# Hybrid trunk on one core: level operands of the recurrence kept side by side, the small-tile scores gathered into two visits a round, the first microseconds reordered

## The chip, the core and the metric

The kernel runs on one core of a Trainium2 chip. The metric is the device time of one execution in microseconds. Three runs of the kernel before took 986.7 to 988.48 us, median 987.43. One more execution was recorded by the hardware profiler; all rows below are of that one.

## What is computed

Two decoder layers over 256 tokens of 2048 features. The change touches the first, a gated linear recurrence (HGRN2) with 16 heads of 128:

```python
def hgrn2_mixer(h, w_in, lb, head_gain, w_out):
    proj = (h @ w_in).astype(jnp.float32).reshape(B, S, 4, HGRN_HEADS, HGRN_HEAD_DIM)
    q, f_pre, v, z = proj[:, :, 0], proj[:, :, 1], proj[:, :, 2], proj[:, :, 3]
    log_f = jnp.log(lb + (1.0 - lb) * jax.nn.sigmoid(f_pre))
    k = (1.0 - lb) * jax.nn.sigmoid(-f_pre)
    o = chunk_gated_recurrence(q * HGRN_HEAD_DIM ** -0.5, k, v, log_f)
    o = rms_norm(o, head_gain) * jax.nn.silu(z)
    return o.reshape(B, S, HGRN_WIDTH).astype(h.dtype) @ w_out
```

Within the recurrence the output at token t is the sum over s <= t of (q_t . decay(s, t) . k_s) v_s, where decay(s, t) is the product of the gates between s and t, one per feature. The second layer (sparse attention with three branches) and the final norm are not touched.

## The kernel before

**Main products.** Every weight matrix is streamed once from HBM in pieces of 128 x 1024 numbers (L26). SyncE issues the loads into six buffers; ScalarE casts a piece to fp32r (`hi`, L132), VectorE subtracts that from the raw piece (`lo`, L142), and TensorE multiplies hi and lo parts with hi and lo parts of the activations (L150 token-major, three products a term; L173 and L175 feature-major). A piece gives twelve token-major products of 512 columns, or eight feature-major pairs.

**The order of work.** It is written out by hand. `plan` lists the pieces of all chunks; `flush` (L252) walks through it: a piece's products, and before and after them one `advance()`, which takes one step of every open generator in `steps` (a `yield` ends a step). So a generator makes two steps a piece, and its instructions stand in each engine's queue between those of the pieces. `prefetch` emits casts, splits and loads some pieces ahead. In the first chunk, whose pieces have `before` set, `start_piece` (L240) does that, with `split_x` (L318): it transposes a 256-column block of x on TensorE and makes its hi and lo part on ScalarE and VectorE. `flush` begins with `start_piece(2)` and asks in the middle of piece i for piece i + 3. Pieces 0 and 1 hold one row block of the weights each and share the first block of x; from piece 2 on each piece needs a block of its own, the last being piece 8.

**Before flush** (L1110 to L1132): seven small loads of parameters into `prow` and `rb` on POOL's queue, x and the first pieces on SyncE's, a transpose of the norm gains `gn` (L1125), `start_piece(0)`, ten transposes of the identity into an unused bank (L1129), then the generators `setup()` (masks, bias table, lower bounds `lb` and `oml`) and `norm_x()`.

**A round of the recurrence** has four heads, worked as two pairs (a = 0, 1), and streams four chunks of eight pieces: f, q, v, z. At the end of each f chunk `f_take` (L423) moves the four result banks out; the first time it calls `open_hg` (L581), which drains all open generators and hands the memory of the start to the recurrence, so `gather`'s copies wait for the last reader of that memory.

**Scores** (`scores_of`, L473), started for both pairs when q is done, so during the v chunk. It goes over levels h = 1, 2, 4 ... 128. A level's products give the scores between neighbouring blocks of h tokens; then q of every second block and k of every other are multiplied in place with the gates `T` of the neighbouring block (L514, L515) and the gates pairwise with each other (L519). For h up to 16 (L491) the products are 32 x 32 tiles, placed with `tile_position` in four column groups of the array, sixteen for each pair and level; the first level takes 64 moving columns (two levels of q at once). Level 32 (L497) has eight products in two of the four column groups, level 64 (L502) four products with a 64-column stationary, level 128 (L506) two with full tiles. A level's products come at the end of a piece, its multiplications at the beginning of the next, so a round has eight visits of TensorE to them, each with both pairs one behind the other. VectorE picks the results by masks (L523, L526); ScalarE and POOL copy them to `ST` (L529, L533, L535, L537), which `mix_of` (L540) multiplies with v after the z chunk.

Matmul records of the trace: a float32 product leaves two loads and two matmuls.

Of the kernel before, what the change touches and what calls it, by code (L numbers as in the profile page):

```python
# [8 lines left out]
F32 = mybir.dt.float32  # L9
# [7 lines left out]
P = 128  # L17
D = 2048
S = 256
KT = D // P  # L20
NH = 16
HD = 128
# [23 lines left out]
def kernel(ctx: ExitStack, tc: tile.TileContext, x, norm_gains, final_gain, rel_bias,  # L46
                             hgrn_lb, hgrn_w_in, hgrn_head_gain, hgrn_w_out, nsa_w_in, nsa_pe_k, nsa_pe_v,
                             phi_k_w1, phi_k_b1, phi_k_w2, phi_v_w1, phi_v_b1, phi_v_w2, nsa_w_out, out):
    nc = tc.nc
# [190 lines left out]
    def start_piece(i):  # L240
        while state["hi"] <= min(i, len(plan) - 1):
            j = state["hi"]
            ch, kts, _ = plan[j]
            if ch and ch["before"]:
                ch["before"](kts)
            prefetch(j, 1)
            while state["lo"] <= j:
                emit_lo(state["lo"])
                state["lo"] += 1
            prefetch(j, 0)  # L250

    def flush():  # L252
        start_piece(2)
        finished = None
        for i, (ch, kts, last) in enumerate(plan):
# [10 lines left out]
            emit_products(i, (lambda: start_piece(i + 3)) if starting else None)  # L266
# [42 lines left out]
    xt = sp.tile([P, 2, D], F32, name="xt")  # L309
    ssqp = sp.tile([P, 2, 4], F32, name="ssqp")  # L310
# [39 lines left out]

    def setup():
# [26 lines left out]
        nc.gpsimd.tensor_copy(xf, xi)  # L378
        yield
# [7 lines left out]
        yield  # L387
        yield
        yield
# [83 lines left out]
    def scores_of(a):  # L473
        Fg, Kg, QQ = HG["F", a], HG["K", a], HG["Q", a]
        ST, S32 = HG["ST", a], HG["S32", a]
        nc.vector.tensor_mul(QQ[:, 1], QQ[:, 0], Fg)
        TT = HG["pool"].tile([P, 512], F32, tag=f"TT{a}", name="TT")
        T, off = Fg, 0
        yield
        lev = []  # L480
        for l, h in enumerate((1, 2, 4, 8, 16, 32, 64, 128)):
            if h <= 16:
                i0, i1 = (0, 2) if l == 0 else (l + 1, l + 2)
                if h in (1, 8):
                    lev.append(aux_bank().rearrange("p (l j t) -> p l j t", l=4, j=4))
                dst = lev[i0 // 4]
                q0 = 0 if l == 0 else 1
                for j in range(4):
                    for b in range(4):
                        cs = slice(j * P + 32 * b, j * P + 32 * b + 32)  # L490
                        nc.tensor.matmul(dst[32 * b:32 * b + 32, i0 % 4:(i1 - 1) % 4 + 1, j, :], Kg[:, cs],  # L491
                                         QQ[:, q0:2, cs], start=True, stop=True, tile_position=(0, 32 * b))
            elif h == 32:
                for j in range(4):
                    for b in (0, 2):
                        c = j * P + 32 * b
                        nc.tensor.matmul(lev[1][32 * b:32 * b + 32, 2, j, :], Kg[:, c:c + 32],  # L497
                                         QQ[:, 1, c + 32:c + 64], start=True, stop=True, tile_position=(0, 32 * b))
            elif h == 64:
                far = aux_bank()  # L500
                for j in range(4):
                    nc.tensor.matmul(far[0:64, j * 64:j * 64 + 64], Kg[:, j * P:j * P + 64],  # L502
                                     QQ[:, 1, j * P + 64:j * P + 128], start=True, stop=True)
            else:
                for hh in range(2):
                    nc.tensor.matmul(far[:, 256 + hh * P:256 + (hh + 1) * P], Kg[:, hh * S:hh * S + P],  # L506
                                     QQ[:, 1, hh * S + P:(hh + 1) * S], start=True, stop=True)
            yield
            if h < 128:
                n = 512 // (2 * h)  # L510
                Tv = T.rearrange("p (n two) -> p n two", two=2)
                Qv = QQ[:, 1].rearrange("p (n two h) -> p n two h", two=2, h=h)
# [652 lines left out]
```

## Time and profile before

| | us |
|---|---|
| median of three runs | 987.43 |
| lowest, highest | 986.7, 988.48 |
| the profiled execution | 988.16 |
| its span, first to last instruction | 986.3 |
| busy in it: PE, DVE, ACT, POOL | 968.3, 658.1, 543.7, 52.4 |

The span lies 1.86 us under the execution's own time; what stands around it is not in the trace. PE is TensorE's matmul, PEld its weight load, DVE VectorE, ACT ScalarE, POOL GpSimd. Matmuls are pipelined: a record's duration is longer than the distance to the next, so prices are taken from the distances.

### The profile page before, as it was taken

To read this page: it belongs to the slowest core of one execution; us is meant where nothing else is said; L and a number is where in the kernel's file an instruction comes from. 1 tells how busy PE (TensorE), PEld (TensorE's weight loads), DVE (VectorE), ACT (ScalarE), POOL (GpSimd) and SP (SyncE) were. 2 spreads that over 40 slices of the span, in tenths; PEclk is the share of its full clock that TensorE was granted. 3 is DMA by queue.
4 is the path that set the end of the run, shared out by engine and by line. 5 is a ranking of instruction groups with operands and counts; after the bars stand their busy time and mean duration, and the time that the engine had idled before them with its cause. 6 is when DMAs were issued, how large, how long until landed. Compare 5 with 4: busy or idle time off the path is not lost.

```text
span 986.3 us, 17479 instructions
## 1 busy us (share of the span) xinstructions
PE 968.3 (98%) x6721; PEld 836.3 (85%) x6721; DVE 658.1 (67%) x1274; ACT 543.7 (55%) x976; POOL 52.4 (5%) x154
## 2 busy tenths in 40 slices
PE   7999999999999999999999999999999999999996
PEld 6888888888888887888888898998899889888886
DVE  5778376846784678365556766455787888786654
ACT  6734563446344634455545655445777877875442
POOL 3101000100010001000011000000000000000000
PEclk9999999999999999999999999999999999999999
DMA  9555565555556555667777666574454445457662
GB/s 316 179 162 174 159 190 152 171 170 176 166 158 186 165 165 154 201 186 243 236 223 227 197 213 192 165 242 162 138 162 130 149 129 151 149 164 239 204 214 98
DMA packets 102612, 178.98 MB, mean 181 GB/s; under 512 B 6016, under 2 KB 25056, under 8 KB 102400
## 3 DMA queue, kind: packets, MB, share of 16 engines
q1 hardware_dynamic: 100512, 171.86, 56.8%
q0 software_dynamic: 1680, 5.46, 1.7%
q8 instruction: 53, 0.87, 0.4%
q10 hardware_dynamic: 336, 0.54, 0.1%
q14 instruction: 31, 0.25, 0.1%
HBM read 173.62 MB, written 4.22 MB: 180 GB/s over the span
## 4 chain that ended last, share of the span: by engine, by line
PE 92%; ACT 3%; DVE 2%; issue 1%; DMA 1%; SPq 0%; POOL 0%; DVEq 0%; POOLq 0%; ACTq 0%
PE mainps L150 40%; PE mainps L173 28%; PE mainps L175 14%; PE auxps L150 4%; PE auxps L491 2%; ACT L L900 1%; DVE lo L142 1%; DMA xt<-in_x_dram 1%; ACT hi L132 1%; PE auxps L920 1%; PE auxps L326 0%; PE auxps L502 0%; PE auxps L549 0%; PE auxps L550 0%; PE auxps L506 0%
## 5 line engine op out<-in xcount | busy, mean ns | idle before, releaser
L132 ACT CAST hi<-raw 128x1024 fp32r<-128x1024 f32 (+3 forms) x317 | 328.6, 1040 | 288.7 <-PE mainps L150 176.2
L142 DVE TENSOR_TENSOR lo<-raw,hi 128x1024 fp32r<-128x1024 f32 (+3 forms) x317 | 380.1, 1208 | 160.4 <-ACT hi L132 158.8
L173 PE MATMUL mainps<-xx,hi 128*128 128x512 f32 x1280 | 455.3, 398 | 4.1 <-DVE zs L303 3.2
L175 PE MATMUL mainps<-xx,lo 128*128 128x256 f32 x1280 | 357.6, 279 | 0.0
L173 PEld LDWEIGHTS mainps<-xx,hi 128*128 128x128 f32 x1280 | 240.8, 188 | 59.1 <-DVE zs L303 4.1
L175 PEld LDWEIGHTS mainps<-xx,lo 128*128 128x128 f32 x1280 | 241.8, 189 | 0.2
L150 PE MATMUL mainps<-hi,xx 128*128 128x512 f32 (+1 forms) x704 | 211.8, 377 | 0.0
L150 PEld LDWEIGHTS mainps<-hi,xx 128*128 128x128 f32 x704 | 128.4, 188 | 23.2
L150 PE MATMUL mainps<-lo,xx 128*128 128x512 f32 (+1 forms) x352 | 130.8, 372 | 0.0
L150 PE MATMUL mainps<-hi,yh 128*128 128x512 f32 (+1 forms) x288 | 105.9, 368 | 0.0
L150 PE MATMUL mainps<-hi,yl 128*128 128x512 f32 (+1 forms) x288 | 105.3, 366 | 0.0
L150 PE MATMUL mainps<-lo,yh 128*128 128x512 f32 (+1 forms) x288 | 105.3, 366 | 0.0
L150 PEld LDWEIGHTS mainps<-lo,xx 128*128 128x128 f32 x352 | 66.1, 188 | 10.1
L150 PEld LDWEIGHTS mainps<-hi,yl 128*128 128x128 f32 x288 | 54.3, 189 | 8.7
L150 PEld LDWEIGHTS mainps<-lo,yh 128*128 128x128 f32 x288 | 54.4, 189 | 8.6
L150 PEld LDWEIGHTS mainps<-hi,yh 128*128 128x128 f32 x288 | 54.4, 189 | 8.5
L900 ACT ACTIVATE L<-L,mx 128x128 f32<-128x128 f32 (+1 forms) x96 | 37.5, 393 | 23.4 <-DVE mx L895 23.4
L303 DVE TENSOR_TENSOR zs<-mainps,zs 128x256 f32<-128x256 f32 x48 | 18.7, 420 | 13.2 <-ACT zs L301 12.2
L533 POOL COPY ST<-S 32x128 f32<-32x128 f32 x32 | 14.6, 455 | 226.4 <-DVE S L526 225.2
L893 DVE CUSTOM_DVE_ANT_0 L<-auxps,bias 128x128 f32<-128x128 f32 (+1 forms) x96 | 22.0, 291 | 3.4 <-PE auxps L150 2.7
L938 DVE TENSOR_TENSOR pl<-auxps,ph 128x512 fp32r<-128x512 f32 (+1 forms) x32 | 17.3, 554 | 9.8 <-ACT ph L934 8.4
L564 DVE SCALAR_TENSOR_TENSOR y<-auxps,rs,sz 128x128 f32<-128x128 f32 x32 | 9.0, 344 | 22.2 <-POOL rs L79 22.2
(243 smaller groups left out, 859.3 us busy)
## 6 DMA issues: line engine op xcount, KB each, us to landing
raw<-in_hgrn_w_in_dram SPq DMA_DIRECT2D x127, 512.0 KB, 3.9
raw<-in_nsa_w_in_dram SPq DMA_DIRECT2D x104, 512.0 KB, 3.8
raw<-in_hgrn_w_out_dram SPq DMA_DIRECT2D x32, 512.0 KB, 4.8
raw<-in_nsa_w_out_dram SPq DMA_DIRECT2D x32, 512.0 KB, 4.4
raw<-in_nsa_w_in_dram SPq DMA_DIRECT2D x10, 420.0 KB, 3.4
xt<-in_x_dram SPq DMA_DIRECT2D x8, 256.0 KB, 8.4
raw<-in_x_dram SPq DMA_DIRECT2D x4, 512.0 KB, 4.0
x_dram<-x POOLq DMA_DIRECT2D x4, 512.0 KB, 6.2
```

What stands on the lines that cost most here:

```text
L132: nc.scalar.copy(hi[:, :m], raw[:, :m])
L142: nc.vector.tensor_sub(lo[:, :m], raw[:, :m], hi[:, :m].bitcast(F32))
L150: nc.tensor.matmul(dst, a, b, start=first and n == 0, stop=last and n == 2, skip_group_check=True)
L173: nc.tensor.matmul(ps, hv[:, fs], xx[:, k].rearrange("p a t -> p (a t)"), start=k == 0, stop=False, skip_group_check=True)
L175: nc.tensor.matmul(ps[:, S:], lv[:, fs], xh[:, k], start=False, stop=k == KT - 1, skip_group_check=True)
L303: nc.vector.tensor_add(o, p[:, :S], o)
L491: nc.tensor.matmul(dst[32 * b:32 * b + 32, i0 % 4:(i1 - 1) % 4 + 1, j, :], Kg[:, cs], QQ[:, q0:2, cs], start=True, stop=True, tile_positio ...
L533: nc.gpsimd.tensor_copy(ST[rs, :, 0:3:2, rs], S32[rs].rearrange("p (h t) c -> p h t c", h=2))
L893: nc.vector.tensor_tensor_reduce(out=dst, in0=lg, in1=b, op0=ALU.add, op1=ALU.max, scale=1.0, scalar=-3e38, accum_out=mx[:, i:i + 1])
L900: nc.scalar.activation(dst, dst, AF.Exp, bias=mx[:, i:i + 1], accum_out=sm[:, i:i + 1])
L920: nc.tensor.transpose(t1[:, i * P:(i + 1) * P], l[:, c0:c0 + P], ident)
L938: nc.vector.tensor_sub(pl[:, ks, hh, :], t, ph[:, ks, hh, :].bitcast(F32))
```

## The change

Three things. In `scores_of` the operands of three levels are kept in separate tiles: `QL` and `KL` join `QQ` and `Kg`, VectorE writes a level's multiplied half to the next set and ScalarE copies the other half there. The products of levels 1 to 4 then run in one visit (`near`), those of levels 8 to 32 in a second (`mid`). Level 64 takes a 128-column stationary instead of 64. In the start, piece 0's cast and split go ahead of its part of x, the lookahead is one piece shorter, and the parameter loads move into `setup`, which gets two steps more. Ahead of the gains' transpose TensorE multiplies seven tiles of zeros, and the ten transposes of the identity become six float32 products of it.

```diff
@@ start_piece, flush
-            if ch and ch["before"]:
+            starting = ch and ch["before"]
+            if starting and j:
                 ch["before"](kts)
             prefetch(j, 1)
             while state["lo"] <= j:
                 emit_lo(state["lo"])
                 state["lo"] += 1
+            if starting and not j:
+                ch["before"](kts)
             prefetch(j, 0)
...
-        start_piece(2)
+        start_piece(1)
...
-            emit_products(i, (lambda: start_piece(i + 3)) if starting else None)
+            emit_products(i, (lambda: start_piece(i + 2)) if starting else None)
@@ start
+    zeros = sp.tile([P, P], F32, name="zeros")
+    nc.vector.memset(zeros, 0.0)
...
+    def load_parameters():
+        nc.gpsimd.dma_start(prow[0:48, 0, :], hgrn_lb.rearrange("a (h d) -> (a h) d", d=HD))
...
@@ setup
         nc.gpsimd.tensor_copy(xf, xi)
+        load_parameters()
...
         nc.gpsimd.tensor_copy(masks, mf)
-        yield
-        yield
-        yield
+        for _ in range(5):
+            yield
@@ scores_of
...
+        TT = pool.tile([P, 512], F32, tag=f"TT{a}", name="TT")
+        QL = pool.tile([P, 2, 512], F32, tag=f"QL{a}", name="QL")
+        KL = pool.tile([P, 2, 512], F32, tag=f"KL{a}", name="KL")
+        Q1 = QQ[:, 1]
+        sets = [(Q1, Kg), (QL[:, 0], KL[:, 0]), (QL[:, 1], KL[:, 1])]
+        chain = {"T": Fg, "off": 0}
+        def to_next(h, src, dst):
+            n = 512 // (2 * h)
+            Tv = chain["T"].rearrange("p (n two) -> p n two", two=2)
+            for x, y, half in ((src[0], dst[0], 1), (src[1], dst[1], 0)):
+                xv, yv = (z.rearrange("p (n two h) -> p n two h", two=2, h=h) for z in (x, y))
+                nc.vector.tensor_mul(yv[:, :, half], xv[:, :, half],
+                                     Tv[:, :, 1 - half:2 - half].to_broadcast([P, n, h]))
+                if src is not dst:
+                    nc.scalar.copy(yv[:, :, 1 - half], xv[:, :, 1 - half])
+            if h < 64:
+                off = chain["off"]
+                Tn = TT[:, off:off + n]
+                nc.vector.tensor_mul(Tn, Tv[:, :, 0], Tv[:, :, 1])
+                chain["T"], chain["off"] = Tn, off + n
+        def small_tiles(dst, q, k, cols=32):
+            for j in range(4):
                 for b in range(4):
+                    cs = slice(j * P + 32 * b, j * P + 32 * b + 32)
+                    qs = q[:, cs] if cols == 32 else QQ[:, 0:2, cs]
+                    nc.tensor.matmul(dst[32 * b:32 * b + 32, j] if cols == 32 else dst[32 * b:32 * b + 32, :, j],
+                                     k[:, cs], qs, start=True, stop=True, tile_position=(0, 32 * b))
+        def lev_bank():
+            return aux_bank().rearrange("p (l j t) -> p l j t", l=4, j=4)
+        def pick(levels, bank):
+            for n, i in enumerate(levels):
+                nc.vector.copy_predicated(S32, masks[:, i, None, :].to_broadcast([P, 4, 32]), bank[:, n])
+        nc.vector.tensor_mul(Q1, QQ[:, 0], Fg)
+        yield
+        to_next(1, sets[0], sets[1])
+        yield
+        yield
+        to_next(2, sets[1], sets[2])
+        yield
+        yield
+        near = lev_bank()
+        small_tiles(near[:, 0:2], Q1, Kg, 64)
+        small_tiles(near[:, 2], *sets[1])
+        small_tiles(near[:, 3], *sets[2])
+        yield
+        pick(range(4), near)
+        yield
+        to_next(4, sets[2], sets[0])
+        yield
+        yield
+        to_next(8, sets[0], sets[1])
+        yield
+        yield
+        to_next(16, sets[1], sets[2])
+        yield
+        yield
+        mid = lev_bank()
+        small_tiles(mid[:, 0], *sets[0])
+        small_tiles(mid[:, 1], *sets[1])
+        Q5, K5 = sets[2]
+        for j in range(4):
+            for b in (0, 2):
+                c = j * P + 32 * b
+                nc.tensor.matmul(mid[32 * b:32 * b + 32, 2, j, :], K5[:, c:c + 32], Q5[:, c + 32:c + 64],
+                                 start=True, stop=True, tile_position=(0, 32 * b))
+        yield
+        pick((4, 5), mid)
+        for b in (0, 2):
+            rs = slice(32 * b, 32 * b + 32)
+            nc.scalar.copy(ST[rs, :, 0:3:2, 32 * b + 32:32 * b + 64],
+                           mid[rs, 2].rearrange("p (h t) c -> p h t c", h=2))
+        for b in range(4):
+            rs = slice(32 * b, 32 * b + 32)
+            nc.gpsimd.tensor_copy(ST[rs, :, 0:3:2, rs], S32[rs].rearrange("p (h t) c -> p h t c", h=2))
+        yield
+        to_next(32, sets[2], sets[2])
+        yield
+        yield
+        far = aux_bank()
+        for j in range(4):
+            nc.tensor.matmul(far[:, j * 64:j * 64 + 64], K5[:, j * P:(j + 1) * P], Q5[:, j * P + 64:(j + 1) * P],
+                             start=True, stop=True)
+        yield
+        to_next(64, sets[2], sets[2])
+        yield
+        for hh in range(2):
+            nc.tensor.matmul(far[:, 256 + hh * P:256 + (hh + 1) * P], K5[:, hh * S:hh * S + P],
+                             Q5[:, hh * S + P:(hh + 1) * S], start=True, stop=True)
+        yield
+        nc.scalar.copy(ST[0:64, :, 0:3:2, 64:128], far[0:64, 0:256].rearrange("p (h t c) -> p h t c", h=2, t=2))
+        nc.vector.tensor_copy(ST[:, :, 1, :], far[:, 256:512].rearrange("p (h c) -> p h c", h=2))
@@ the loads and the end
-    nc.gpsimd.dma_start(prow[0:48, 0, :], hgrn_lb.rearrange("a (h d) -> (a h) d", d=HD))
...
+    def keep_busy(n, m):
+        for _ in range(n):
+            nc.tensor.matmul(gp[:, 256:256 + P], m, m, start=True, stop=True)
+
+    keep_busy(7, zeros)
     nc.tensor.transpose(gp[:, :32], gn, ident[:32, :32])
     nc.vector.tensor_copy(gcol, gp[:, :32])
     start_piece(0)
-    for i in range(10):
-        nc.tensor.transpose(gp[:, 256:256 + P], ident, ident)
+    keep_busy(6, ident)
     run(setup())
```

## Rows read from the trace of the kernel before

**Rows 1.** The page's first part: busy us, share of the span, instructions.

```profile
PE 968.3 (98%) x6721; PEld 836.3 (85%) x6721; DVE 658.1 (67%) x1274; ACT 543.7 (55%) x976; POOL 52.4 (5%) x154
```

**Rows 2.** The chain that ended last, in order of time: start us, us, what.

```profile
2.20 6.80 DMA xt<-in_x_dram
...
63.81 1.23 PE auxps L491 x64
...
67.99 0.69 PE auxps L491 x50
68.69 2.93 PE mainps L150 x12
...
82.47 0.63 PE auxps L497 x32
...
86.05 1.07 PE auxps L502 x16
87.12 2.95 PE mainps L150 x12
...
90.07 0.89 PE auxps L506 x8
90.96 21.77 PE mainps L150 x96
```

**Rows 3.** Windows over the scores' stretch, round 0: us, then busy us by engine.

```profile
61.07:92.20 31.13, 31.13 (x479) 24.55 (x479) 28.47 (x69) 12.38 (x18) 3.62 (x8) 1.00 0.46 129
```

**Rows 4.** Timeline of two score visits and of L798: start us, us, engine, line.

```profile
63.79 1.25 PE L491 MATMUL auxps<-QQ,Kg 128*32 128x64 f32 x64
...
67.92 0.76 PE L491 MATMUL auxps<-QQ,Kg 128*32 128x32 f32 x64
...
564.91 0.31 PEld L798 LDWEIGHTS auxps<-scratch 128*128 128x128 f32 x2
```

**Rows 5.** Groups by line and shape, TensorE matmul (PE) and weight load (PEld): busy us, mean ns.

```profile
L491 PE MATMUL auxps<-QQ,Kg 128*32 128x32 f32 x1024 | 12.2, 199 | 0.0
...
L506 PEld LDWEIGHTS auxps<-QQ,Kg 128*128 128x128 f32 x32 | 4.2, 191 | 0.3
...
L502 PEld LDWEIGHTS auxps<-QQ,Kg 128*64 128x64 f32 x64 | 4.0, 138 | 1.4 <-issue 1.4
```

**Rows 6.** Groups by line and shape, DVE and ACT, first 540 us: busy us, mean ns.

```profile
L142 DVE TENSOR_TENSOR lo<-raw,hi 128x1024 fp32r<-128x1024 f32 x174 | 211.1, 1223 | 95.0 <-ACT hi L132 94.2
...
L514 DVE TENSOR_TENSOR QQ<-QQ,TT 128x256 f32<-128x256 f32 x48 | 20.8, 433 | 3.3 <-PE auxps L491 2.4 <-PE auxps L497 0.9
...
L132 ACT CAST hi<-raw 128x1024 fp32r<-128x1024 f32 x175 | 183.7, 1052 | 184.2 <-PE mainps L150 117.3 <-PE mainps L173 56.4 <-DVE TT L519 10.3
...
L301 ACT COPY QQ<-mainps 128x256 f32<-128x256 f32 x16 | 5.9, 371 | 3.3 <-PE mainps L175 3.3
```

**Rows 7.** Timeline of the first microseconds: start us, us, engine, line.

```profile
1.92 0.69 POOL L1111 DMA_DIRECT2D prow<-in_hgrn_lb_dram  x1 [0.30 <-POOL prow L1110]
...
4.87 2.34 PE L1129 MATMUL auxps<-ident 128*128 128x128 f32 x10
...
9.81 0.78 PE L173 MATMUL mainps<-xx,hi 128*128 128x512 f32 x1
...
15.10 0.39 PE L173 MATMUL mainps<-xx,hi 128*128 128x512 f32 x1
```

**Rows 8.** Windows of the first microseconds; the last columns are granted clock, DMA share, GB/s.

```profile
4.00:4.50 0.50, 0.50 (x3) 0.50 (x4) 0.11 (x1) 0.00 (x0) 0.50 (x2) 1.00 1.06 362
4.50:5.00 0.50, 0.50 (x4) 0.50 (x3) 0.00 (x0) 0.00 (x0) 0.50 (x2) 1.00 0.58 199
```

**Rows 9.** Timeline where the first f chunk ends and q begins: start us, us, idle before.

```profile
34.67 0.17 DVE L410 TENSOR_TENSOR lbs<-lbe 128x16 f32<-128x16 f32 x1
...
35.58 0.17 DVE L414 TENSOR_SCALAR oml<-lb 128x16 f32<-128x16 f32 x1
...
38.39 0.50 PE L173 MATMUL mainps<-xx,hi 128*128 128x512 f32 x1 [0.68 <-DVE Kg L303]
```

More of the change, by code (lines that the diff above doesn't have):

```diff
@@ L349 @@
     rb = sp.tile([BUCKETS, NH], F32, name="rb")
+    def load_parameters():
+        nc.gpsimd.dma_start(prow[0:48, 0, :], hgrn_lb.rearrange("a (h d) -> (a h) d", d=HD))
+        nc.gpsimd.dma_start(prow[48:49, 0, :], hgrn_head_gain)
+        nc.gpsimd.dma_start(prow[49:50, 0, :], phi_k_b1)
+        nc.gpsimd.dma_start(prow[50:51, 0, :], phi_v_b1)
+        nc.gpsimd.dma_start(prow[0:32, 1, :], nsa_pe_k[0])
+        nc.gpsimd.dma_start(prow[32:64, 1, :], nsa_pe_v[0])
+        nc.gpsimd.dma_start(rb, rel_bias)
     def setup():
@@ L473, in scores_of @@
     def scores_of(a):
+        pool = HG["pool"]
         Fg, Kg, QQ = HG["F", a], HG["K", a], HG["Q", a]
         ST, S32 = HG["ST", a], HG["S32", a]
-        nc.vector.tensor_mul(QQ[:, 1], QQ[:, 0], Fg)
-        TT = HG["pool"].tile([P, 512], F32, tag=f"TT{a}", name="TT")
-        T, off = Fg, 0
-        yield
[L480 to L512, printed above, removed]
-                Kv = Kg.rearrange("p (n two h) -> p n two h", two=2, h=h)
-                nc.vector.tensor_mul(Qv[:, :, 1], Qv[:, :, 1], Tv[:, :, 0:1].to_broadcast([P, n, h]))
-                nc.vector.tensor_mul(Kv[:, :, 0], Kv[:, :, 0], Tv[:, :, 1:2].to_broadcast([P, n, h]))
-                if h < 64:
-                    Tn = TT[:, off:off + n]
-                    off += n
-                    nc.vector.tensor_mul(Tn, Tv[:, :, 0], Tv[:, :, 1])
-                    T = Tn
-            if h == 4:
-                for i in range(4):
-                    nc.vector.copy_predicated(S32, masks[:, i, None, :].to_broadcast([P, 4, 32]), lev[0][:, i])
-            elif h == 32:
-                for i in range(4, 6):
-                    nc.vector.copy_predicated(S32, masks[:, i, None, :].to_broadcast([P, 4, 32]), lev[1][:, i - 4])
-                for b in (0, 2):
-                    rs = slice(32 * b, 32 * b + 32)
-                    nc.scalar.copy(ST[rs, :, 0:3:2, 32 * b + 32:32 * b + 64],
-                                   lev[1][rs, 2].rearrange("p (h t) c -> p h t c", h=2))
-                for b in range(4):
-                    rs = slice(32 * b, 32 * b + 32)
-                    nc.gpsimd.tensor_copy(ST[rs, :, 0:3:2, rs], S32[rs].rearrange("p (h t) c -> p h t c", h=2))
-            elif h == 128:
-                nc.scalar.copy(ST[0:64, :, 0:3:2, 64:128],
-                               far[0:64, 0:256].rearrange("p (h t c) -> p h t c", h=2, t=2))
-                nc.vector.tensor_copy(ST[:, :, 1, :], far[:, 256:512].rearrange("p (h c) -> p h c", h=2))
-            yield
@@ new lines, in scores_of @@
+        yield
[4 more added lines that the diff above has]
+                           mid[rs, 2].rearrange("p (h t) c -> p h t c", h=2))
+        for b in range(4):
+            rs = slice(32 * b, 32 * b + 32)
[3 more added lines that the diff above has]
+        yield
@@ L1110 @@
     nc.gpsimd.memset(prow, 0.0)
-    nc.gpsimd.dma_start(prow[0:48, 0, :], hgrn_lb.rearrange("a (h d) -> (a h) d", d=HD))
-    nc.gpsimd.dma_start(prow[48:49, 0, :], hgrn_head_gain)
-    nc.gpsimd.dma_start(prow[49:50, 0, :], phi_k_b1)
-    nc.gpsimd.dma_start(prow[50:51, 0, :], phi_v_b1)
-    nc.gpsimd.dma_start(prow[0:32, 1, :], nsa_pe_k[0])
-    nc.gpsimd.dma_start(prow[32:64, 1, :], nsa_pe_v[0])
-    nc.gpsimd.dma_start(rb, rel_bias)
     for c in range(8):
```

## The prediction

> **What bounds the kernel now.** The page's first part comes first: the matmuls of TensorE (PE) fill 98% of the span, VectorE (DVE) 67%, ScalarE (ACT) 55% [rows 1]. So PE's own order of work sets the end, and a change pays only by taking time out of that order or by closing one of its few gaps. The chain of waits then tells where the touched work lies in it. In each of the four rounds it runs through PE alone: twelve main products, a short visit to the score products, twelve main products, and so on, eight visits a round [rows 2]. Ninety-six undisturbed main products take 21.77 us, so twelve take 2.72. Behind a visit to the small tiles the twelve take 2.93, behind L502 2.95: a visit costs its own time and 0.21 to 0.23 us of a late restart. The windows over that stretch show why the other engines matter here: PE is full, and DVE is busy 28.5 of 31.1 us, ACT only 12.4 [rows 3]. The start is another regime: the chain begins with 6.80 us of waiting for the second column block of x, and the first main product stands behind it.
>
> **The change part by part: scores.** Old price of a round: the first visit 1.23 + 0.21 = 1.44; four of 0.69 + 0.21 = 0.90; L497 0.63 + 0.21 = 0.84; L502 1.07 + 0.23 = 1.30; L506 0.89 with nothing behind it [rows 2]. Sum 8.07 us.
>
> What part of a visit is products, and what is the switch? Each product leaves two matmul records (32 products, 64 records). In the 32-column visit the last record starts 0.76 - 0.20 = 0.56 us after the first, 9 ns a record; in the 64-column visit, whose records last 0.02 longer, (1.25 - 0.22)/63 = 16 ns [rows 4, 5]. So 64 records at 9 ns are 0.58 us and 0.32 us of the 0.90 are fixed. L497 fits: half its column groups are empty, so it keeps the 16 ns, 32 x 16 = 0.51, plus 0.32 = 0.83 against 0.84.
>
> The new near visit holds for both heads pairs 64 records of 64 columns and 128 of 32: 1.02 + 1.15 + 0.32 = 2.49. The mid visit holds 128 full and 32 half-empty records: 1.15 + 0.51 + 0.32 = 1.98. Together 4.47 for 5.88: the same records, four fixed prices fewer, and 0.13 of the first visit's excess. That is 1.41 a round, **5.6 us** in four.
>
> L502 becomes a product with a 128-column stationary, of whose rows half are unused. Its weight load lasts 191 ns as L506's does, where 64 columns took 138 [rows 5]; the 64 moving columns no longer cover it. The nearest row is L798, the same shape: its two loads take 0.31 us, so the second starts 0.12 behind the first [rows 4]. L506's eight records at 0.89/8 = 111 ns carry the same load; I take that: 16 x 0.111 = 1.78 against 1.30, **1.9 us lost** in four rounds. Ends: 16 x 67 ns = 1.07 if the load hides (0.9 gained in four), 16 x 0.12 + 0.23 = 2.15 if an exit price stays as well (3.4 lost).
>
> The Trainium skill speaks against this part too: TensorEngine Tiling (Array Packing), section When to Use Tiling, has a stationary of 64 columns or fewer use two column tiles, for up to twice the speed. By that rule undoing it would take 1.07 to 2.14 us, and the loss would be 3.4. But the trace shows no such overlap to lose: L502's records stand 67 ns apart, four times the 16 ns of the visit that does use four column groups, since all of them name the same tile. So the sum stays with the load.
>
> Net for the scores: 5.6 - 1.9 = 3.7 us. L506's visit keeps its 0.89.
>
> **What lies beside PE.** The level products on DVE are the same in number and shape, only written to other tiles, at about 0.43 us each, or 0.34 from one start to the next [rows 6]. They come in lumps now: a level's six products (1.6 to 2.0 us) and a split of 1.22 us are 2.8 to 3.2 us for a piece of 2.72. I followed DVE's queue from the start of the v chunk, in us from there: q's scaling and the first multiplication end at 3.3 (four operations of 0.64 after ACT's last copies), a split at 4.5, level 1 for both pairs (six starts at 0.34) at 6.5, a split at 7.7, level 2 (its gate products are shorter, 1.75) at 9.4. PE begins the near visit after three pieces, at 8.2, with the first pair, and comes to the second pair's third set only near 10: no wait. The visit ends at 10.7; eight selections at about 0.31 run to 13.2, a split to 14.4, level 4 (1.6) to 16.0, a split, level 8 (1.5) to 18.7, a split, level 16 to 21.4, when PE comes to the mid visit after four more pieces (21.6). Each split is done 1 to 2 us ahead of its piece, which follows two pieces behind. DVE is late nowhere, by 0.2 us at the closest, so I cost it at nothing; without that cover each late level would stop PE directly. ACT gets ten copies for each heads pair, 80 in all. The nearest row is 0.37 us for 128x256 [rows 6]; four of them and a cast of 1.05 are 2.5 us of a piece of 2.72, so casts end later but still two pieces ahead. Behind a copy that waits for DVE stand ACT's casts, and behind those DVE's splits. The scores last two pieces longer, into the z chunk, and the mixing that reads them starts only at its end: nothing.
>
> **The start.** Now the first main product runs at 9.81, and for 0.78 us, twice the 0.39 of 15.10, where piece 2 starts [rows 7]: the array is still at the lower of its two levels (1.2 GHz), after 9 us in which PE ran ten transposes and little else, though the windows print a granted clock of 1.00 [rows 8]. Seven products of zeros are 14 records; at 2.34/10 = 0.234 us they fill PE to about 4.2, and gn's transpose moves 0.6 us. The cast and split of piece 0 now go ahead of x's, and with one piece less of lookahead PE is asked for the second block only in the middle of piece 0: its products can start near 7.0, at the higher level (2.4 GHz). The seven small loads leave POOL's queue, where they began at 1.92, for step 7 of setup, near 15 us: at 0.69 us each they hold it for up to 4.8 us, ahead of the cast of the masks, which nothing wants before the scores, and landing as slowly as x's second block, 6.8 us, they are there at 27, a microsecond before PE transposes them. Between 4.0 and 5.0 the DMA rate fell from 362 to 199 GB/s while they ran; two such microseconds are 0.3 MB, so the second block of x may land 0.9 us sooner, at 8.1. From there: four transposes at 0.111 (128 columns, as L506's), four pairs at 0.34 (one and a half of 0.227), four transposes, two pairs: 11.0; but piece 2's split is done only near 11.7, after x's part (1.4 from the transposes), a cast of 1.05 and 1.22. So piece 2 starts near 11.7 instead of 15.10, **3.4 us**.
>
> Most of it is given back where q begins. q's banks wait for the drain of setup and norm: today PE idles 0.68 there [rows 9]. Setup is two steps longer, so its last five DVE operations (34.67 to 35.75, 1.1 us) fall into that drain, behind the last split, and its Exp stands ahead of the cast of piece 10 on ACT. From the transposes of the last block of x, in the middle of piece 6, to q's first product the path is: x's part, cast and split of piece 8, 3.2 us; the two copies of parameters 0.75; split of piece 9 1.2; three operations on the bounds 0.6; Exp 0.25; cast and split of piece 10 2.25; the last five operations 1.1; sum, POOL, ACT's first copy and DVE's first addition 1.3. That is 10.7 us. PE has half a piece (1.4), the parameters' transposes (1.0) and two pieces at 2.8, 8.0 us. It idles 2.7 instead of 0.7, so 2.0 go back. Start: 3.4 - 2.0 = **1.4 us**; ends 3.4 gained (no waiting at q) and 0.7 lost (block lands as today and the drain is as long).
>
> Sum: 3.7 + 1.4 = 5.1 us. The profiled execution took 988.16, its span 986.3; it becomes 983.1. The three runs' median is 987.43, 0.73 under it: **982.3**.
>
> **The rivals.**
> *Casts fall behind* (0.14). If a copy with a stride costs twice its 0.37, four copies and a cast are 4.0 us for a piece of 2.72: 1.3 behind on each of five levels, 6.5, less the two pieces of lead, 5.4, is 1.1 a round, 4.4 in all: 986.7. For: no row has a strided ACT copy. Against: DVE's products at stride two take no longer than the others [rows 6].
> *The switch is paid inside a visit* (0.11), so that the change doesn't do what it says: near alternates 64 and 32 columns three times, 3 x 0.32 a round, 3.8 in all: 986.1. Against: two heads pairs already share a visit at one pitch.
> *Instruction supply* (0.12), the slower end. The near visit is 384 instructions (192 loads, 192 matmuls), the mid 320; no stretch today has more than 128. Those 128 ran in 0.76 us, 5.9 ns each [rows 4], but half may have been queued before. Then 64 took 0.69, 10.8 ns each, and 320 + 256 of them would take 6.2 us where the products need 3.8: 2.4 a round, 9.6 in all: 991.9, slower. It decides from 8.9 ns on. The Trainium skill, Runtime: NRT & Kernel Launch, section Instruction fetch mechanics, names a floor of about 20 cycles an instruction, 8.3 ns at the higher and 16.7 ns at the lower of the two levels (an estimate from that page): by it the end would be 986 to 1005. The trace's 5.9 ns lies below both.
>
> **How the numbers follow.** Forecast 0.63; by itself 979.5 to 985.2 (far part and start at their ends). The rivals as given. The range 978.5 to 988.0 leaves out the supply case and a little below. A measurement of this kernel tells some 0.2%, 2 us, from no change: faster is the forecast and a sliver of the two middle rivals, 0.65; within 0.2% 0.22; slower 0.13.
>
> **What would show it.** Right: two visits of about 2.2 and 1.7 us in the chain instead of six, no DVE or ACT named before them; L502's successor near 1.8; first main product near 7, q's start near 37, with a gap of over 2 us before it. Wrong: near's records further apart than 9 and 16 ns (supply); ACT's casts waiting on DVE with PE idle behind (casts); no gap before q (start undersold).

## The result, and the profile after

The changed kernel took 992.93 us in the median of six runs (991.09 to 996.60), the kernel before 988.04 beside it (986.70 to 989.12): a ratio of 1.0053, 95 % interval 1.0033 to 1.0073. It is slower by about 5 us, where 982.3 was forecast. The profiled execution took 993.81, its span 992.0.

The page of after, parts 1, 3 and 4 (part 1 of before is [rows 1]):

```profile
PE 970.0 (98%) x6737; PEld 844.5 (85%) x6737; DVE 658.2 (66%) x1275; ACT 570.5 (58%) x1056; POOL 56.8 (6%) x154
...
q8 instruction: 53, 0.87, 0.4%
...
PE 91%; ACT 3%; DVE 3%; issue 2%; DMA 0%; POOL 0%; POOLq 0%; DVEq 0%; ACTq 0%
```

ACT's 80 copies are there, and PE is as full as before by its share. New is "issue": time on the chain in which PE waited for nothing that the profile shows. The waits of PE in after (waited for: us in total, times, longest):

```profile
PE auxps L520 <- issue: 3.5, 2, 2.6
PE mainps L150 <- issue: 3.2, 1, 3.2
PE mainps L173 <- DVE zs L306: 3.2, 4, 1.7
PE mainps L173 <- DVE Kg L306: 2.1, 1, 2.1
```

Three stretches of idle time, 6.7 us, at the new visits (L520 and L561 are their products, L150 the main products behind them), and none of them put down to VectorE or ScalarE. The chain shows where they lie, and the first round has none (start us, us, what; that of before is [rows 2]):

```profile
61.62 8.22 PE mainps L150 x36
69.84 2.24 PE auxps L520 x178
72.08 11.10 PE mainps L150 x48
...
85.05 5.65 PE mainps L150 x24
90.70 1.73 PE auxps L578 x16
92.43 2.82 PE mainps L150 x12
95.25 0.89 PE auxps L584 x8
```

This is the forecast's round: near 2.24, mid 1.87 (83.18 to 85.05), level 64 at 1.73, level 128 at 0.89, and no wait. The second round:

```profile
168.64 1.79 PE auxps L520 x135
170.43 0.87 issue
171.30 0.63 PE auxps L520 x40
171.93 11.13 PE mainps L150 x48
...
184.60 0.29 PE auxps L561 x15
184.89 3.22 issue
188.12 2.29 PE mainps L150 x5
```

The same products, with 0.87 us of nothing inside the near visit and 3.22 right behind the mid one. The third stretch, 2.63 us, stands twelve records ahead of the end of the third round's near visit, at 275.40. The fourth round has none.

The granted clock is the second thing that the page's average hides. Windows of after (us; busy us of PE, PEld, DVE, ACT and POOL with counts; PEclk; DMA share; GB/s):

```profile
36.00:38.00 2.00, 0.99 (x5) 0.88 (x6) 1.42 (x4) 1.87 (x5) 1.92 (x5) 0.91 0.71 236
38.00:40.00 2.00, 2.00 (x8) 1.71 (x8) 1.23 (x1) 1.22 (x2) 1.10 (x3) 0.50 0.12 36
40.00:42.00 2.00, 2.00 (x11) 1.72 (x10) 0.13 (x1) 0.46 (x1) 0.00 (x0) 0.73 0.58 155
...
188.00:190.00 2.00, 1.89 (x5) 1.50 (x5) 1.77 (x4) 0.00 (x0) 1.85 (x3) 0.50 0.76 236
190.00:192.00 2.00, 2.00 (x7) 1.58 (x7) 0.00 (x0) 0.19 (x1) 0.00 (x0) 0.69 0.48 90
```

After 2.1 us of idle PE ahead of q, and again after the 3.22 us, the products run for a while at the lower level (1.2 GHz). The second fall makes 24 main products last 7.09 us instead of 5.65, 1.4 more. The first spoils the start: q begins at 37.01 [rows 9], 1.38 us earlier than before, as forecast (1.4), but v's first product comes at 61.46, before at 60.90.

The ledger between the two profiled executions, +5.7: start +0.6, idle stretches +6.7, second clock fall +1.4, and -3.5 from rounds that without a stretch are 0.87 us shorter (98.80 from the first near visit to the second, before 99.67 on average from first visit to first visit). That makes 5.2. The other 0.5 lies in the second and third round: from near visit to near visit they take 104.57 and 101.71 us, together 8.7 more than twice 98.80, of which the two rounds' stretches and the clock fall are 8.1.

### The profile page after: what moved, and what is told of

Read it like the earlier page. It is cut to its first block, busy times and chain, and to the rows that moved or that the text cites. A ratio compares the mean times of both kernels' runs of the same rounds, so it can differ in the third digit from the quotient of the medians.

```text
span 992.0 us, 17669 instructions
## 1 busy us (share of the span) xinstructions
PE 970.0 (98%) x6737; PEld 844.5 (85%) x6737; DVE 658.2 (66%) x1275; ACT 570.5 (58%) x1056; POOL 56.8 (6%) x154
## 4 chain that ended last, share of the span: by engine, by line
PE 91%; ACT 3%; DVE 3%; issue 2%; DMA 0%; POOL 0%; POOLq 0%; DVEq 0%; ACTq 0%
PE mainps L150 40%; PE mainps L173 27%; PE mainps L175 14%; PE auxps L150 4%; PE auxps L520 1%; DVE lo L142 1%; ACT L L950 1%; ACT hi L132 1%; PE auxps L578 1%; PE auxps L970 1%; PE auxps L1170 1%; DMA raw<-in_hgrn_w_in_dram 0%; PE auxps L599 0%; PE auxps L600 0%; PE auxps L584 0%
## 5 line engine op out<-in xcount | busy, mean ns | idle before, releaser
L150 PE MATMUL mainps<-hi,xx 128*128 128x512 f32 (+1 forms) x704 | 208.3, 375 | 3.2 <-issue 3.2
L150 PEld LDWEIGHTS mainps<-hi,xx 128*128 128x128 f32 x704 | 129.1, 189 | 22.9
L150 PE MATMUL mainps<-lo,xx 128*128 128x512 f32 (+1 forms) x352 | 131.4, 373 | 0.0
L150 PE MATMUL mainps<-hi,yh 128*128 128x512 f32 (+1 forms) x288 | 105.9, 368 | 0.0
L150 PE MATMUL mainps<-hi,yl 128*128 128x512 f32 (+1 forms) x288 | 105.3, 366 | 0.0
L150 PE MATMUL mainps<-lo,yh 128*128 128x512 f32 (+1 forms) x288 | 105.3, 366 | 0.0
L150 PEld LDWEIGHTS mainps<-lo,xx 128*128 128x128 f32 x352 | 66.5, 189 | 13.9 <-issue 3.1
L150 PEld LDWEIGHTS mainps<-hi,yl 128*128 128x128 f32 x288 | 54.3, 189 | 8.8
L150 PEld LDWEIGHTS mainps<-hi,yh 128*128 128x128 f32 x288 | 54.4, 189 | 8.6
L150 PEld LDWEIGHTS mainps<-lo,yh 128*128 128x128 f32 x288 | 54.4, 189 | 8.4
L571 POOL COPY ST<-S 32x128 f32<-32x128 f32 x32 | 19.1, 598 | 232.3 <-DVE S L528 231.0
```

The source lines that it names most:

```text
L150: nc.tensor.matmul(dst, a, b, start=first and n == 0, stop=last and n == 2, skip_group_check=True)
L571: nc.gpsimd.tensor_copy(ST[rs, :, 0:3:2, rs], S32[rs].rearrange("p (h t) c -> p h t c", h=2))
```

## Experiments

Theory: **supply**. TensorE's instructions come in packets on the queue marked q8, 53 of 16 KB for 6737 matmuls and 6737 loads, so 254 instructions a packet. While PE works through one the next is fetched, and a packet used up faster than that makes PE wait. The rivals: a wait on data that the profile doesn't name, the price of switching the array's tiles, or something the new start does.

### The two parts alone, and two ways to move the packets' ends

If a packet is 256 instructions, one count of the program in that size puts the three stretches at one place: in the second round's near visit a packet ends 288 instructions in (of 384), at the mid one 320 in (of 320), in the third round's near one 368 in. By the trace's records PE stopped 292, 320 and 360 in. The same count gives the other five visits a first end at 144 to 240 and the next one past their end. A round has 1712 instructions, 80 short of seven packets, so the place moves from round to round.

**e1_start_only**: `scores_of` is that of before.

```diff
-        near = lev_bank()
-        small_tiles(near[:, 0:2], Q1, Kg, 64)
...
+        for l, h in enumerate((1, 2, 4, 8, 16, 32, 64, 128)):
```

> The start of after with the scores of before. Supply theory (TensorE's instructions come in packets, 53 for 6737 matmuls and 6737 weight loads, 254 of them each; a visit to the small array tiles that uses up a whole packet in under about 5 us stops for the next one): visits are 128 instructions here, so no idle time called issue near the scores. The start alone is then to be seen: the product of q starts 1.4 us earlier than before, but TensorE idles 2.1 us ahead of it and the granted clock falls to the lower level for some 3 us, which costs about 1.9: 988.5, within 1 us of before. Rival (the start is a plain gain, and all of the loss is the scores'): 986.6. Rival (the start carries the whole loss): 993.

Measured 987.62 (987.36 to 990.64), before 988.28, ratio 1.0000 (0.9992 to 1.0009). No "issue" anywhere in PE's waits. The loss isn't the start's. In its profile the clock did not fall, though PE idled 2.1 us ahead of q there too: q begins at 36.73 and v at 59.65, 1.25 us ahead of before.

**e2_scores_only**: the start is that of before, `scores_of` that of after.

```diff
-    keep_busy(7, zeros)
...
-    keep_busy(6, ident)
+    for i in range(10):
+        nc.tensor.transpose(gp[:, 256:256 + P], ident, ident)
```

> The scores of after with the start of before. Supply theory: this start has 32 TensorE instructions fewer ahead of the first round, so the packets' ends fall elsewhere in the visits. Counted from the program, with the three idle stretches of after put at one place of a packet: one visit only, the near one of the second round, holds a whole packet with its end inside (some 320 of its 384 instructions in), and so one idle stretch of about 3 us there, perhaps with a stretch at the lower clock behind it (1.4); the mid of the second round and the near of the third run without one. 988.0 less 3.5 for the scores, plus 3 to 4.5: 987.5 to 989. Rival (the idle time is a wait on data or on the switch of tiles): stretches at the same three places as in after, 991 to 993. Rival (the idle time has to do with the start): no stretch, 984.5.

Measured 992.24, ratio 1.0043 (1.0027 to 1.0059): the scores carry the loss. Second and third round of e2 on PE's timeline (start us, us, what, idle before):

```profile
171.02 0.52 PE L506 MATMUL auxps<-QL,KL 128*32 128x32 f32 x32
174.50 0.46 PE L506 MATMUL auxps<-QL,KL 128*32 128x32 f32 x31 [2.96 <-issue]
...
275.94 0.39 PE L150 MATMUL mainps<-hi,xx 128*128 128x512 f32 x1
278.15 0.40 PE L150 MATMUL mainps<-hi,xx 128*128 128x512 f32 x1 [1.83 <-issue]
```

The first stretch stands where the count had it, 31 records (62 instructions) from the end of the near visit where 64 were foretold, with a clock fall behind it. The second is a miss in size: there a packet ends 16 instructions past the visit, and I had taken those few slow instructions to be enough. They aren't. The time is a miss as well: 987.5 to 989 was expected, and 992.24 lies in the range of the wait on data (991 to 993). What speaks against that rival is the stretches themselves: two where after has three, and neither at a place of after's. The profiled execution comes out at 991.9 from 988.16 less 3.5, 4.8 for the stretches, 1.6 for the clock (48 main products in 12.68 us instead of 11.10) and 0.8 by which v begins later than in before, with the same start; it took 992.99, so 1.1 is left open.

**e3_pad** and **e4_shift**: unused 32 x 32 products at the end of a mid visit.

```diff
+        for n in range(pad):
+            j, b = n // 4 % 4, n % 4
+            cs = slice(j * P + 32 * b, j * P + 32 * b + 32)
+            nc.tensor.matmul(mid[32 * b:32 * b + 32, 3, j], K5[:, cs], Q5[:, cs], start=True, stop=True,
+                             tile_position=(0, 32 * b))
...
-            run(scores_of(0))
-            run(scores_of(1))
+            for a in range(2):
+                run(scores_of(a, (6, 20, 0, 0)[s]))
```

(e4: 10, 0, 0, 0.)

> After with 12 matmuls of 32 x 32 tiles added at the end of the first round's mid visit and 40 at the end of the second round's (results unused): 48 and 160 TensorE instructions more, 104 records at 9 ns, some 0.9 us of added work. Supply theory: they are chosen so that no visit of 384 or 320 instructions holds the end of a packet that lies wholly within its fast stretch; all three idle stretches go (6.7 us), and with the second one the 1.4 us at the lower clock behind it: 992.9 - 8.1 + 0.9 = 985.7. Rival (a wait on data, or the switch): the three stay, and the time is 993.8. Rival (supply, but of the bytes in all): longer visits make it worse, above 994.

> After with 20 matmuls of 32 x 32 tiles at the end of the first round's mid visit (80 TensorE instructions, results unused), which is what one round's count lacks to whole packets. Supply theory: the idle stretches of after move by exactly one round: none in the second round, about 0.9 us inside the near visit of the third (288 instructions in), about 3.2 us behind the mid visit of the third, about 2.6 us in the near visit of the fourth (368 of 384 in); the time stays at 993. Rival (a wait on data, or chance): they stay in the second and third rounds, or lie anywhere.

e3 measured 985.81 (984.42 to 986.90) against the 985.7 expected, ratio 0.9973 (0.9961 to 0.9984): 104 records of added work make the kernel 7 us faster. The waits of PE in e3:

```profile
PE mainps L173 <- DVE zs L306: 3.2, 4, 1.7
PE mainps L173 <- DVE Kg L306: 2.1, 1, 2.1
PE auxps L1175 <- DVE zeros L314: 1.1, 1, 1.1
```

"issue" is gone, and the operands, the data and the switches are all as in after; that excludes the first two rivals. e4 took 992.0 (one run). Its stretches on PE's timeline:

```profile
283.32 0.28 PE L561 MATMUL auxps<-QL,KL 128*32 128x32 f32 x6 [1.99 <-issue]
...
373.43 0.46 PE L520 MATMUL auxps<-QL,KL 128*32 128x32 f32 x18 [2.42 <-issue]
```

The two large stretches have moved one round on, to the end of the third round's mid visit and the end of the fourth round's near one; the second round is clean. The small one (0.9) did not show. Each of the two was followed by a clock fall (granted 0.50 in the windows 285:287 and 374:376), so the sum is nearly that of after.

A whole packet inside a visit is not enough for a wait. By the count e3's second mid visit, 480 instructions with its pads, holds one from 16 to 272, its end being in the first row here. The visit runs through from 180.38 to 182.91, with no idle time:

```profile
181.60 0.43 PE L520 MATMUL auxps<-QQ,Kg 128*32 128x32 f32 x29
...
181.86 0.48 PE L520 MATMUL auxps<-QL,KL 128*32 128x32 f32 x31
```

What goes with the wait is how far into the visit that packet begins. At 16 (e3) and 32 (e4, third near) there is no stretch, at 32 in after one of 0.87; at 64 they are 3.22 (after), 2.96 (e2) and 1.99 (e4), at 112 they are 2.63 (after) and 2.42 (e4). The transfers fit: on the instruction queue of e3 one packet moves between 178.7 and 179.8, before the visit begins, and none from there to its end, so what PE runs behind the packet's end had come by then.

### The price of a packet

**e8_long**: e3's pads, with 512 products more in the first round's mid visit.

```diff
-                run(scores_of(a, (6, 20, 0, 0)[s]))
+                run(scores_of(a, (262, 20, 0, 0)[s]))
```

> The price of a packet by itself: the kernel of e3_pad with 512 more matmuls of 32 x 32 tiles (2,048 TensorE instructions, eight whole packets, so that the later rounds keep their places; results unused) at the end of the first round's mid visit. Supply theory: from the place where TensorE's sequencer reaches a packet to the first instruction of the next one it was 4.4 to 5.1 us in after, so that each of eight packets takes about that: the visit stretches by 35 to 41 us, in lumps of some 256 instructions at 9 ns a record and then 3 to 4 us of idle time: 1020 to 1027. Rival (no limit of supply, only 9 ns a record): 1024 records more, 9.2 us, 995. Rival (a steady rate of 8.9 ns an instruction, as the forecast had it): 18 us, 1004.

Measured 1017.38 (one run, the profiled one), 31.6 above e3's median. In the profiles the round with this visit takes 131.99 us and in e3 98.99, so the longer visit costs 33.0 more. PE's timeline of e8 through that visit:

```profile
87.88 1.91 PE L566 MATMUL auxps<-QL,KL 128*32 128x32 f32 x128 [4.11 <-issue]
91.61 1.93 PE L566 MATMUL auxps<-QL,KL 128*32 128x32 f32 x128 [1.82 <-issue]
...
102.34 1.94 PE L566 MATMUL auxps<-QL,KL 128*32 128x32 f32 x128 [1.68 <-issue]
105.79 1.93 PE L566 MATMUL auxps<-QL,KL 128*32 128x32 f32 x128 [1.52 <-issue]
109.25 1.93 PE L566 MATMUL auxps<-QL,KL 128*32 128x32 f32 x128 [1.52 <-issue]
```

This is the mechanism in the open. Between two idle stretches lie 128 records (127 in one case), which with their loads are 256 instructions, and one round of work and idling takes 3.46 us (105.79 to 109.25). The DMA of the same stretch, 84 to 114 us in 40 slices, has next to nothing but the packets, one pulse every four or five slices of 0.75 us:

```profile
GB/s 385 93 0 0 0 0 22 0 0 0 0 22 0 0 0 0 22 0 0 0 22 0 0 0 0 22 0 0 0 0 22 0 0 0 0 22 0 0 0 0
...
q8 instruction: 8, 0.13, 1.8%
```

Eight packets in 30 us on otherwise idle DMA engines: PE waits for packets without contention from the weights. Whether the weights lengthen the single stretches is not shown; they moved at 373 GB/s in 185.0:185.5, just before the packet of after's longest, and at 385 in e8's first slice here. In e8's steady part a transfer starts 1.0 to 1.2 us after the first record of the packet before it, lasts 0.9 to 1.3, and ends 1.3 to 1.5 ahead of its own first record: the three follow each other, and their sum is the 3.46. I had priced a packet at 4.4 to 5.1 us, from stretches that came out of slow work. The first one here, with its 4.11 us of idle time, is of that size; the later ones follow each other faster, so the visit cost 33.0 and not 35 to 41. (From 88 to 116 the granted clock was 0.50, so the records stand 15 ns apart, and the stretches are part work, part idling.) The Trainium skill, Runtime: NRT & Kernel Launch, section Instruction fetch mechanics, describes the structure: blocks of 16 KiB, 256 instructions, the next fetched while the current one runs. The 128 records agree. It also holds that a floor of about 20 cycles an instruction hides the fetch, a floor of the sequencer's issue (the prediction counted it at the array's two levels). These visits run at 5.8 ns an instruction (2.24 us for 384), under even the smaller of the prediction's two figures (8.3), and 3.46 us a packet is 13.5 ns an instruction. The measurement decides: in these visits the fetch is not hidden.

In after itself the order of events can be bounded: PE stops at 184.89, a packet's transfer lies within 185.80 to 186.90, PE goes on at 188.12; likewise 275.40, 275.70 to 276.70, 278.04. The DMA of those two windows:

```profile
q8 instruction: 1, 0.02, 5.4%
```

```profile
q8 instruction: 1, 0.02, 5.7%
```

So about 1.3 us more pass from the end of a transfer to the first instruction.

### Remedies, and the other terms of the sum

**e6_stagger**: the second pair of heads one piece later.

```diff
-            run(scores_of(1))
+            run(scores_of(1), 1)
```

> After with the second pair of heads one piece behind the first, so that each visit has 192 or 160 TensorE instructions in place of 384 or 320, and there are four visits a round in place of two. No instruction is added. Supply theory: 24 slow instructions lie between two visits, and no packet is used up fast enough to wait: no idle time called issue, 992.9 - 8.1 for the stretches and the lower clock, plus 8 more visits at the forecast's fixed price of 0.32 (2.6): 987.4. Rival (the separate operands or the switch make the idle time): it stays, 993 or more.

Measured 988.78 beside 988.82, ratio 0.9999 (0.9989 to 1.0009). 0.2 us of "issue" are left of 6.7: supply again. It is dearer than the 987.4 expected. With the same main products between, a near visit in two halves takes 0.40 us longer than in one (13.74 for 13.34, first product to the mid visit) and a mid visit 0.41 (7.93 for 7.52, to level 64), not 0.32. Level 64 and level 128 fall apart too, into three visits, but that adds only 0.05 a round. Together 0.86, or 3.4 in four rounds for 2.6; the rest of the 1.4 is open but for the 0.2 of "issue".

**e11_three**: three visits of 256, 256 and 192 instructions, and the narrow operand of e5.

```diff
-        small_tiles(near[:, 3], *sets[2])
         yield
-        pick(range(4), near)
+        pick(range(3), near)
         yield
         to_next(4, sets[2], sets[0])
         yield
         yield
+        next_ = lev_bank()
+        small_tiles(next_[:, 0], *sets[2])
+        small_tiles(next_[:, 1], *sets[0])
+        yield
+        pick((3, 4), next_)
+        yield
         to_next(8, sets[0], sets[1])
...
-        small_tiles(mid[:, 0], *sets[0])
...
-        pick((4, 5), mid)
+        pick((5,), mid[:, 1:])
```

> After with three visits a round of 256, 256 and 192 TensorE instructions in place of two of 384 and 320 (no operation added, no pads), and the narrow operand of e5. Supply theory: no visit holds a whole packet with a slow stretch missing on both sides, so there is no idle time called issue, wherever the packets end; 992.9 - 8.1 (idle stretches and lower clock) - 1.8 (operand) + 4 x 0.32 (one visit more a round) = 984.3. Rival (a visit of 256 still waits): above 987.

Measured 984.10 (981.42 to 985.06), ratio 0.9951 (0.9935 to 0.9966), without pads and without idle time called issue.

**e5_far_narrow**: on e3, level 64 takes its 64 columns again.

```diff
-            nc.tensor.matmul(far[:, j * 64:j * 64 + 64], K5[:, j * P:(j + 1) * P], Q5[:, j * P + 64:(j + 1) * P],
+            nc.tensor.matmul(far[0:64, j * 64:j * 64 + 64], K5[:, j * P:j * P + 64], Q5[:, j * P + 64:(j + 1) * P],
```

> The kernel of e3_pad with the 64-key level's stationary operand narrowed to the 64 columns that are used (as in before); instructions the same in number. The forecast's term: 16 records at 0.111 us (1.78 a round) against 1.30 before, so 0.45 a round, 1.8 in four rounds: 985.8 - 1.8 = 984.0. Rival (the wide stationary operand costs nothing, since the visit's price is its switch): 985.8.

Measured 982.81 (981.70 to 985.19) beside 988.82, ratio 0.9945 (0.9931 to 0.9958). Undisturbed rounds (third near visit to fourth) go from 98.78 in e3 to 98.28: 0.50 a round, 2.0 in four, against the 1.8 expected. The median lies 1.2 under the 984.0 expected, more than the rounds explain.

**e7_params_early**: on e3, the parameter loads right behind the first memsets, three steps in place of five.

```diff
         nc.gpsimd.memset(brow, NEG)
+        load_parameters()
...
-        load_parameters()
...
-        for _ in range(5):
+        for _ in range(3):
```

> The kernel of e3_pad with the loads of the parameters issued some 14 us earlier (behind the first memsets of POOL) and the setup's wait cut from five steps to three, so that the five operations on the bounds leave the drain, where they hold the sum of squares back by 1.0 us. Theory (the drain gives back part of what the start gains, because those five operations stand in it): TensorE's idle time ahead of q falls from 2.1 to about 1.1, 985.8 - 1.0 = 984.8. Rival (something else in the drain is as late): 985.8. Rival (the small loads delay the first blocks of x): 986 to 987.

Measured 986.52 beside 988.82, ratio 0.9979 (0.9968 to 0.9989), e3's 0.9973 within the interval: no gain. VectorE at the drain of e7:

```profile
34.69 0.17 DVE L428 TENSOR_SCALAR oml<-lb 128x16 f32<-128x16 f32 x1
34.80 1.22 DVE L142 TENSOR_TENSOR lo<-raw,hi 128x1024 fp32r<-128x1024 f32 x1
35.94 0.15 DVE L349 TENSOR_REDUCE ssq<-ssqp 128x2 f32<-128x8 f32 x1
```

The five operations are ahead of the drain now, and the split of the next piece has taken their place; the sum of squares comes at 35.94, in e3 at 35.88. The rival holds: removing a late step only brings up the next one. The small loads are not the reason: PE waits 0.8 us for x and in e3 0.3, but piece 2 starts at 11.49, in e3 at 11.62.

**e9_drain_busy, e10_start_busy, e12_three_busy**: on e5 (pads cut to 2 and 20), e1 and e11, eight products of the identity in the drain.

```diff
     def f_take(ps):
         if "pool" not in HG:
+            b = aux_bank()
+            for _ in range(8):
+                nc.tensor.matmul(b[:, :P], ident, ident, start=True, stop=True)
             open_hg()
```

> The kernel of e5_far_narrow with eight matmuls of the identity matrix (128 x 128, results unused) put into TensorE's idle time ahead of the first product of q, and the pads cut so that every packet's end lies as it did. Nothing leaves the path. Theory (the idle time ahead of q lets the granted clock fall in some of the runs, at some 1.9 us each): no stretch at the lower level behind the drain, the runs draw together at the fast end of e5's, 982.0 in the median. Rival (the fall has another cause, or comes by chance): median and spread as in e5, 982.8. Rival (the eight matmuls overrun the idle time): 983.5.

> The kernel of e1_start_only with the same eight matmuls in the drain. Theory (the start's own gain is 1.25 us at the first product of v, part of which the clock's fall takes back in some runs): 1.2 us below before, ratio 0.9988. Rival (the start gains nothing once the clock is held): ratio 1.000.

> The kernel of e11_three with the eight matmuls of e9_drain_busy in TensorE's idle time ahead of q (16 records, 32 instructions, so every packet's end moves by 32 places; one visit of the second round now holds a packet exactly, from its first to its last instruction). Supply theory: still no idle time called issue, since some 45 slow instructions ahead of that visit are taken from the packet's fetch. Theory of the drain: no stretch at the lower clock behind it, so less spread than e11 (981.4 to 985.1) and 983.0 in the median. Rival (a whole packet inside a visit always waits): one idle stretch of 1 to 3 us in the second round, 985. Rival (the clock falls anyway): as e11, 984.1.

The drain of e9 on PE's timeline:

```profile
34.45 1.95 PE L441 MATMUL auxps<-ident 128*128 128x128 f32 x16
36.74 0.50 PE L173 MATMUL mainps<-xx,hi 128*128 128x512 f32 x1 [0.34 <-DVE Kg L306]
```

| | median, range | before beside it | ratio (95 %) |
|---|---|---|---|
| e9 | 982.53 (981.73 to 983.83) | 988.50 | 0.9945 (0.9932 to 0.9959) |
| e10 | 987.70 (987.18 to 987.93) | 988.50 | 0.9993 (0.9985 to 1.0002) |
| e12 | 982.89 (982.36 to 984.62) | 987.68 | 0.9949 (0.9935 to 0.9964) |

e10's eleven runs span 0.75 us where e1's eleven spanned 3.3, so the clock behind the drain may be what made e1's runs differ; that is not shown, as only one run of each was profiled, and neither has the fall. Of nine profiled executions with 2.1 us or more of idle PE there, four show the fall (after, e5, e7, e11) and five don't; of the three with the gap filled, none. The medians hardly move. The start alone is worth about 0.7 us once the clock is held, and the measurement cannot quite tell that from nothing. e12 has one visit that by the count holds a packet exactly, from its first instruction on, and still no "issue" in its waits.

The fastest is e9 (e5 is level with it), which depends on pads laid to this program's count. e12 has no scores pads, is as fast within the intervals, and beats before by about 0.5 % and after by about 1 %.

## Why the prediction was wrong

**The end of a visit, not its price.** "Two visits of about 2.2 and 1.7 us in the chain instead of six, no DVE or ACT named before them": right, 2.24 and 1.87. The net of the scores was put at 3.7 us; undisturbed rounds give 3.5. VectorE and ScalarE came late nowhere in the scores, as costed, so the casts rival falls; and near alternates its column counts at one price, so the switch rival falls too.

**The step that failed is instruction supply, which the sum put at nothing.** It stood outside as a rival. It was given 0.12, a steady rate, and a threshold of 8.9 ns an instruction, and was set against the 5.9 ns of a 128-instruction visit [rows 4]. That row can't speak on supply: 128 instructions are half a packet, and no packet can be used up within them. The real condition is one of lumps: whether a packet is used up faster than its successor comes (3.46 us in e8's steady part, 13.5 ns an instruction; 4 to 5, by an estimate from after's two large stretches). A visit of 384 or 320 instructions can hold a whole packet, one of 128 never. Whether it does, and where in the visit the packet begins, depends on the count of all instructions ahead of it: three of eight visits did in after, and that cost 6.7 us, with 1.4 more at the lower clock. The rival's 991.9 lay near the result, but for another mechanism: by its rate all eight visits would have been slow, and five ran at full speed. What should have moved the chance was on the page of before: 53 packets of instructions for 13,442 matmuls and loads (6721 of each), 254 a packet, smaller than the visits planned.

```profile
q8 instruction: 53, 0.87, 0.4%
```

**Level 64**: 1.78 a round forecast, 1.73 measured; the loss of 1.9 was 2.0 by e5. Right.

**The start**: first product forecast near 7.0, measured 7.44 at once at the higher level; piece 2 at 11.7, measured 11.20 with 0.34 of waiting for its split; idle time ahead of q 2.7, measured 2.1; q's start 37, measured 37.01. The 1.4 came out at q (1.38) with other parts than forecast, which is luck: after leads before by 3.9 us at piece 2 (forecast 3.4), by 2.83 at the last piece of f, and idles 1.4 more at the drain, not 2.0. What was missed is that the idle time has a second price: in after the granted clock fell behind it, and between q's and v's first product lie 24.45 us, in e1 22.92, in before 22.51. In e1, without a fall, the lead is 1.66 at q, 1.25 at v and 0.65 at the end of the profiled span, and the ratio of its runs shows none of it.

**The range** ended at 988.0, with the supply case left outside as the slower end; it is there that the result lies. Its core, 979.5 to 985.2, is not what the named ends add up to either: both parts at their ends give 977.5 to 985.9.

## What to carry to other kernels

Count instructions, not only columns, when small products are gathered: a dense stretch longer than one packet of 256 TensorE instructions (here 128 loads and 128 matmuls) can wait for its own program, in lumps whose place and size move with any edit ahead of it. Keep such stretches at or under a packet, with slower work between them. When a profile shows idle time put down to nothing, look at the instruction queue before looking for a semaphore; a pad that moves the packets' ends tells the two apart in one run.

## What was not expected of the hardware

A fetch of instructions costs PE up to 3.2 us at a time (after) and 4.1 (e8), and 1.5 (e8's steady part) on DMA engines that carry next to nothing else. Adding 52 unused products made a kernel 7 us faster. Where the clock fell, it fell behind idle stretches of 2.0 to 4.1 us, but not behind each: the 2.63 us of after's third round were followed by 1.00, the 1.99 of e4 by a fall. Why one and not the other stays open.
